# Second projection of a gated MLP on one NeuronCore: its seven block products in another order, signs moved into the operands, products of one quadrant added up in PSUM

## The chip, the cores and the metric

One core of a Trainium2 chip runs the whole kernel. The metric is device time in microseconds (us) of one execution. The engines are PE (TensorE: matrix products), DVE (VectorE), ACT (ScalarE), POOL (GpSimd) and SP (SyncE, which here only issues transfers). POOL also issues transfers that add to what is already at their destination. PEld is PE's loading of weights.

## The reference

One transformer layer over 1024 positions and 1024 channels: a norm, an input projection, a pooling mixer and chunked attention, an output projection; then the part that the change touches, and a gate at the end.

```
hn = rmsnorm(h, norm_ffn_g)
gt, val = split(hn @ w_up)                       # D_FF = 2816 each
gt = causal_dwconv(gt, conv_w, conv_b)           # width 3
h  = h + (gelu(gt) * val) @ w_down               # second projection: 2816 -> 1024
hn = rmsnorm(h, norm_ple_g)
h  = h + sigmoid(hn @ w_ple_gate + b_ple_gate) * (p @ w_ple)
out = rmsnorm(h, final_g)
```

## The kernel before, in words

Everything is held transposed: channels on the 128 partitions, positions along the row. H[d] is the residual of channel block d (0 to 7), 1024 positions in two halves HS[0], HS[1]. Each fp32 operand is split into two fp32r parts, hi (rounded, on ACT) and lo (the rest, on DVE), and each product is three matmuls: hi by hi, hi by lo, lo by hi (`mm3`, lines 128 to 130). The split is line 133 (ACT) and line 134 (DVE).

The up projection runs over 22 blocks of 128 of the 2816 channels. Block fi ends with `values_in` and a write of its 128 x 1024 result to the DRAM tensor GD[fi] (L869). Its last block uses the PSUM banks 0 to 3.

The second projection is a 2x2 block product done with seven products in place of eight (Strassen's way): the halves are those of the 22 blocks of the inner dimension, of the 1024 output channels, and of the 1024 positions. A product n is 11 steps (k = 0 to 10); step k multiplies a 128 x 512 weight form by a 128 x 512 form of the intermediate result, for four output blocks j of 128 channels: 4 x 3 = 12 matmuls of 512 columns, added up over k in four PSUM banks (`set_of[n]`). One product is 132 matmuls. The names:

- T(k), B12(k), B22(k): blocks of GD in SBUF (regions R0/R1, R2, R3). T is changed in place by sums on DVE as products go by.
- SW(k): sums of weight blocks in region R4. Its first block is a plain load; each further one is added by a transfer that POOL issues (`grown`, L892). Below, a1(k) is the accumulation that makes SW(k) for product 5, a2(k) the one that turns it into that of product 6, a3(k) that of product 3. Product 7 has weight sums of its own, in the raw buffers in F.
- `w_form` (four) and `g_form` (three): rings of split operands, so step i can be split once step i-4 (weights) or i-3 (the other side) is through PE.
- `raw_buf("w")` is a ring of six buffers for weight blocks, `raw_buf("g")` one of five for blocks of GD, "q" one of four for the gate's weights.

What sets the order: PE runs its instructions in program order. For DVE, ACT, POOL and SP a scheduler fixes the order when the program is built; each engine then runs its list strictly in order, and an instruction whose data is not there holds up all behind it. SP and POOL issue transfers in that order too. A transfer on SP's queue waits until the one eight places ahead has landed (its semaphore is one of eight in turn), so at most eight are under way.

`operands(n, k)` loads what step k of product n needs, six steps ahead (READY); `formed` splits it two steps ahead (FORMED); `behind` makes the sums that follow a split; `taken(n, j, ps)` adds the finished bank j to H. In the kernel before, the order of the products is 1, 2, 5, 6, 7, 4, 3, and the four `taken` of a product stand together right behind its last step:

```python
            if k == NK - 1:
                for j in range(4):
                    taken(n, j, PS[:, set_of[n][j]])
```

During the last products the weights of the gate are loaded and split (`gate_weights`), and the first half of the normalised residual (`weighted2`).

Of the kernel before, what the change touches and what calls it, by code (L numbers as in the profile page):

```python
# [83 lines left out]
def trunk(tc, xT, pT, vecs, w_qk0, w_in, w_v, bias, counts, pool_w, w_out, w_up, w_down,  # L84
# [4 lines left out]
    with tc.tile_pool(name="sb", bufs=1) as sb, \  # L89
# [795 lines left out]
        def gated(k, i, j):  # L885
            return GD[k + NK * (i - 1), :, (j - 1) * 512:j * 512]
# [20 lines left out]
        def U(j):  # L907
            return r(56 + 2 * j, 512)

        def operands(n, k):  # L910

            if n == 1:
                return load_to(raw_buf(), weight(k, 1, 1)), load_to(T(k), gated(k, 1, 1))
            if n == 2:
                load_to(B12(k), gated(k, 1, 2))
                return load_to(raw_buf(), weight(k, 1, 2)), load_to(raw_buf("g"), gated(k, 2, 1))
            if n == 5:
                load_to(B22(k), gated(k, 2, 2))
                grown(load_to(SW(k), weight(k, 2, 1)), k, 2, 2)
                return SW(k), T(k)  # L920
            if n == 6:
                return SW(k), T(k)
            if n == 7:
                t = grown(load_to(raw_buf(), weight(k, 2, 1)), k, 1, 1)
                b21[k] = load_to(raw_buf("g"), gated(k, 2, 1))
                return t, B12(k)
            if n == 4:
                return load_to(raw_buf(), weight(k, 2, 2)), T(k)
            return SW(k), load_to(raw_buf("g"), gated(k, 2, 2))

        def behind(n, k):

            tt = dve.tensor_tensor
            if n == 2:
                tt(T(k), T(k), B12(k), ALU.add)
            elif n == 5:
                tt(T(k), T(k), B22(k), ALU.subtract)
                grown(SW(k), k, 1, 1)
            elif n == 6:
                tt(B12(k), B12(k), B22(k), ALU.subtract)  # L940
                grown(SW(k), k, 1, 2)
            elif n == 7:
                tt(T(k), T(k), b21.pop(k), ALU.subtract)

        pinned, b21 = [False], {}
        sequence = [(n, k) for n in (1, 2, 5, 6, 7, 4, 3) for k in range(NK)]
        READY, FORMED = 6, 2
# [7 lines left out]
        def formed(upto):  # L955
            while made[1] < min(upto, len(sequence)):
                i = made[1]
                w_, g_ = got.pop(i)
                split(g_, *g_form[i % 3])
                split(w_, *w_form[i % 4])  # L960
                behind(*sequence[i])
                made[1] += 1
# [11 lines left out]
        rings["g"] = [r(b, 512) for b in range(118, 128, 2)]  # L974


        wg = []
# [14 lines left out]
        norm_b = Norm(HS[1], f(52.25, 512), [f(54.25, 512)], 4, 1)  # L992
# [10 lines left out]
        def taken(n, j, ps):  # L1003

            if n == 1:
                act.activation(U(j), ps, AF.Copy)
            elif n == 2:
                h_add(j, 0, ps)
                norm_a.add(j)
            elif n == 5:  # L1010
                h_add(4 + j, 1, ps)
                h_add(j, 1, ps, ALU.subtract)
            elif n == 6:
                dve.tensor_tensor(U(j), U(j), ps, ALU.subtract)
                h_add(j, 1, U(j), ALU.subtract)
            elif n == 7:
                dve.tensor_tensor(U(j), U(j), ps, ALU.add)
                h_add(4 + j, 0, U(j), ALU.subtract)
                h_add(4 + j, 1, U(j))
                norm_b.add(4 + j)  # L1020
            elif n == 4:
                h_add(4 + j, 0, ps, ALU.subtract)
                norm_a.add(4 + j)
            else:
                h_add(j, 1, ps)
                norm_b.add(j)

        set_of = {1: (0, 1, 2, 3), 2: (0, 1, 2, 3), 5: (4, 5, 6, 7), 6: (0, 1, 2, 3), 7: (4, 5, 6, 7),
                  4: (0, 1, 2, 3), 3: (7, 4, 5, 6)}

        def all_weights():
            for z in (2, 3):
                Rs[z] = region(z, F32R)
            wg.extend(r(32 + 8 * k, 2048) for k in range(KT))

        def first_half_forms():
            for z in (0, 1):
                Rs[z] = region(z, F32R)
            hp[0] = [(r(4 * k, 512), r(4 * k + 2, 512)) for k in range(KT)]

        extra = {(7, 10): all_weights, (4, 10): first_half_forms,
                 (3, 5): norm_a.sums, (3, 7): lambda: norm_a.rows(rst2[:, HS[0]])}
        for k, at in enumerate(((4, 1), (4, 3), (4, 5), (4, 7), (4, 9), (3, 1), (3, 3), (3, 4))):
            extra[at] = lambda k=k: gate_weights(k)

        for i, (n, k) in enumerate(sequence):
# [3 lines left out]
            for j in range(4):  # L1050
                js = slice(j * P, (j + 1) * P)
                mm3(PS[:, set_of[n][j]], whi[:, js], wlo[:, js], ghi, glo, k == 0 and n != 2, k == NK - 1, n == 2)
            if k == NK - 1:
                for j in range(4):
                    taken(n, j, PS[:, set_of[n][j]])
            if (n, k) in extra:
                extra[n, k]()
            if n == 3 and 1 <= k <= 8:
                weighted2(0, k - 1)
# [6 lines left out]
        Rs[4] = region(4, F32R)  # L1066
        pt = [(r(96 + 8 * k, 1024), r(100 + 8 * k, 1024)) for k in range(2)]
        wp = [(r(112 + 8 * k, 1024), r(116 + 8 * k, 1024)) for k in range(2)]
# [48 lines left out]
        for i in range(NG * KT):  # L1117
            g, d = i // KT, i % KT
            gate_mm(d, g, (7, 2, 3)[i % 3])
# [8 lines left out]
            for z in ((0, 1) if i == 1 else (i,)):  # L1128
                gz, dz = z // KT, z % KT
                ple_mm(dz, gz, ple_banks[z % 2])  # L1130
                gate_out(dz, gz, (7, 2, 3)[z % 3], ple_banks[z % 2], zt[z % 4])
# [63 lines left out]
```

## Time and profile before

| | |
|---|---|
| median of 3 runs | 1157.6 us (1156.49 to 1161.36) |
| the profiled execution | 1160.69 us, its span 1158.6 us |
| PE busy over the span | 1129.9 us (98%) |
| DVE, ACT, POOL busy | 902.0, 583.5, 250.5 us |
| clock of PE granted, mean | 0.993 |
| second projection, first to last matmul | 802.45 to 1031.8 us of the span |

The timeline lists instructions by their start; the bracket at a row's end gives the idle time ahead of it and what ended that. Rows that follow one another on DVE overlap a little: a row reads 0.69 us, while four in a row take 2.49. A row of several equal instructions carries their number (x2). The view by windows gives, for each stretch of time, its length and the busy time of each engine with the number of instructions.

### The profile page before, as it was taken

The page shows a single profiled execution, that of the slowest core. Times are in us where ns is not written, and L with a number is a line of the kernel's source. Part 1 is how long each engine was busy: PE and PEld are TensorE (multiplying, and loading weights), DVE is VectorE, ACT ScalarE, POOL GpSimd, SP SyncE. Part 2 cuts the span into 40 slices and gives each one's busy share as a digit, 9 for nine tenths or more (in the row PEclk, how much of TensorE's full clock was granted, in tenths as well). Part 3 has the DMA queues.
Part 4 walks back from the last instruction along what each step waited for, and adds up shares of the span by engine and source line. Part 5 has one row for each costly group of instructions (what it writes and reads, how often), then busy time and mean ns, then how long its engine had stood idle before and what let it go on. Part 6 is the DMA issues. An engine that isn't in the chain of part 4 may idle for free.

```text
span 1158.6 us, 15610 instructions
## 1 busy us (share of the span) xinstructions
PE 1129.9 (98%) x5697; PEld 956.1 (83%) x5697; DVE 902.0 (78%) x1408; ACT 583.5 (50%) x1023; POOL 250.5 (22%) x224
## 2 busy tenths in 40 slices
PE   8999999999999999999999999998999999999996
PEld 7988998888888778888888888887877777888996
DVE  7678878779557678999998999998669767984554
ACT  8568677764655444343434343444534435773332
POOL 0000000083012213343434343332023420000000
PEclk9999999999999999999999999999999999999998
DMA  7110102104510352212131312123999894610011
GB/s 262 37 49 30 49 12 67 39 28 157 171 28 10 69 145 77 103 62 102 64 103 64 105 64 101 64 101 109 322 295 255 149 223 127 209 47 1 26 66 56
DMA packets 58828, 117.22 MB, mean 101 GB/s; under 512 B 6656, under 2 KB 8960, under 8 KB 58752
## 3 DMA queue, kind: packets, MB, share of 16 engines
q1 hardware_dynamic: 50544, 101.48, 25.8%
q0 software_dynamic: 8064, 14.68, 7.6%
q8 instruction: 44, 0.72, 0.3%
q14 instruction: 32, 0.26, 0.1%
q10 hardware_dynamic: 144, 0.07, 0.0%
HBM read 100.48 MB, written 15.73 MB: 100 GB/s over the span
## 4 chain that ended last, share of the span: by engine, by line
PE 81%; issue 6%; DVE 4%; DMA 4%; ACT 2%; POOL 1%; SPq 0%; DVEq 0%; POOLq 0%; ACTq 0%
PE PS L129 24%; PE PS L128 24%; PE PS L130 24%; PE PS L366 2%; DMA R<-GD 2%; PE PS L384 1%; PE PS L383 1%; POOL R L892 1%; DMA R<-in_w_down 1%; DVE B L134 1%; DMA F<-in_w_up 1%; PE PS L341 1%; PE PS L340 1%; DVE F L1001 0%; DMA F<-in_w_qk 0%
## 5 line engine op out<-in xcount | busy, mean ns | idle before, releaser
L128 PE MATMUL PS<-R,R 128*128 128x512 f32 (+1 forms) x896 | 346.3, 386 | 3.1 <-ACT V L796 1.7
L130 PE MATMUL PS<-R,R 128*128 128x512 f32 (+1 forms) x896 | 343.2, 383 | 0.0
L129 PE MATMUL PS<-R,R 128*128 128x512 f32 x832 | 324.9, 390 | 0.3 <-DVE R L229 0.3
L134 DVE TENSOR_TENSOR R<-F,R 128x512 fp32r<-128x512 f32 (+1 forms) x214 | 190.6, 898 | 23.5 <-ACT R L133 22.9
L133 ACT ACTIVATE R<-F 128x512 fp32r<-128x512 f32 (+1 forms) x218 | 132.3, 621 | 140.9 <-PE PS L129 82.3
L128 PEld LDWEIGHTS PS<-R,R 128*128 128x128 f32 x896 | 168.6, 188 | 34.8 <-ACT V L796 2.1
L130 PEld LDWEIGHTS PS<-R,R 128*128 128x128 f32 x896 | 168.5, 188 | 33.5 <-DVE R L134 0.5
L710 POOL TENSOR_TENSOR F<-F 128x512 f32<-128x512 f32 x76 | 143.2, 1884 | 221.4 <-DVE R L134 142.4
L129 PEld LDWEIGHTS PS<-R,R 128*128 128x128 f32 x832 | 156.6, 188 | 31.1 <-DVE R L229 0.9
L129 PE MATMUL PS<-B 128*128 128x512 f32 x316 | 125.3, 396 | 8.8 <-DVE B L134 8.8
L128 PE MATMUL PS<-B 128*128 128x512 f32 x316 | 124.8, 395 | 3.1 <-DVE V L821 2.1
L130 PE MATMUL PS<-B 128*128 128x512 f32 x316 | 124.3, 393 | 0.0
L133 ACT ACTIVATE B<-R 128x512 fp32r<-128x512 f32 x110 | 65.1, 620 | 40.2 <-DMA R<-in_w_down 20.6
L134 DVE TENSOR_TENSOR B<-R,B 128x512 fp32r<-128x512 f32 x110 | 72.6, 687 | 14.4 <-ACT B L133 14.3
L129 PEld LDWEIGHTS PS<-B 128*128 128x128 f32 x316 | 60.1, 190 | 24.9 <-DVE B L134 12.5
L128 PEld LDWEIGHTS PS<-B 128*128 128x128 f32 x316 | 60.0, 190 | 16.9 <-DVE V L821 2.6
L129 PE MATMUL PS<-B,R 128*128 128x256 f32 x256 | 72.3, 282 | 0.0
L130 PEld LDWEIGHTS PS<-B 128*128 128x128 f32 x316 | 60.0, 190 | 12.5
L133 ACT ACTIVATE B<-F 128x512 fp32r<-128x512 f32 (+1 forms) x53 | 35.1, 663 | 67.6 <-PE PS L129 49.2
L352 ACT ACTIVATE F<-F,small 128x640 f32<-128x640 f32 (+2 forms) x64 | 44.4, 693 | 21.1 <-DVE small L350 12.8
L128 PE MATMUL PS<-B,R 128*128 128x256 f32 x192 | 54.6, 285 | 0.0
L130 PE MATMUL PS<-B,R 128*128 128x256 f32 x192 | 54.4, 283 | 0.0
(165 smaller groups left out, 1965.4 us busy)
## 6 DMA issues: line engine op xcount, KB each, us to landing
F<-in_w_up SPq DMA_DIRECT2D x91, 256.0 KB, 2.7
R<-GD SPq DMA_DIRECT2D x66, 256.0 KB, 5.3
GD<-F SPq DMA_DIRECT2D x22, 512.0 KB, 2.6
F<-in_w_down SPq DMA_DIRECT2D x44, 256.0 KB, 5.2
R<-in_w_down POOLq DMA_DIRECT2D x33, 256.0 KB, 6.7
F<-in_w_in SPq DMA_DIRECT2D x10, 512.0 KB, 3.8
F<-in_xT SPq DMA_DIRECT2D x16, 256.0 KB, 6.0
F<-in_w_out SPq DMA_DIRECT2D x16, 256.0 KB, 2.9
```

What stands on the lines that cost most here:

```text
L128: pe.matmul(ps, ahi, bhi, start=first, stop=False, skip_group_check=more)
L129: pe.matmul(ps, ahi, blo, start=False, stop=False, skip_group_check=more)
L130: pe.matmul(ps, alo, bhi, start=False, stop=last, skip_group_check=more)
L133: act.activation(hi, src, AF.Copy)
L134: dve.tensor_tensor(lo, src, rv(hi), ALU.subtract)
L340: pe.matmul(PS[:, 4 + z, 0:320], q, K2[:, ks], start=True, stop=False)
L341: pe.matmul(PS[:, 4 + z, 0:320], q, K1[:, ks], start=False, stop=True)
L352: act.activation(S[:, 0:n], S[:, 0:n], AF.Exp, bias=s_[:, 0:1], scale=-1.0, accum_out=s_[:, 1:2])
L366: pe.transpose(pst[:, j * P:(j + 1) * P], S[:, j * P:(j + 1) * P], ident)
L383: pe.matmul(O, V[:, k, h], pt[:, 0, idx], start=n_ == 0, stop=False)
L384: pe.matmul(O, V[:, k, h], pt[:, 1, idx], start=False, stop=n_ == len(ks) - 1)
L710: pool.tensor_tensor(rawu[to], rawu[a], rawu[b], op)
```

## The change: what it does

1. The order of the products is 1, 5, 6, 3, 7, 2, 4. The halves of the positions are swapped in what GD block is called 1 or 2, so the sums go to other quadrants of H.
2. Products 6, 7 and 4 go on adding in the banks 4 to 7 that product 1 began, product 3 in the banks 0 to 3 that product 5 began (`on_top`): their first matmul doesn't clear the bank. Where a quadrant needs a product with the other sign, the operand is split with a factor of -1 (`split_neg`, products 5 and 6).
3. Each finished bank is added to H once: 28 additions on DVE in place of 40, and no copy by ACT; the four of a product are written behind the steps 1, 3, 5 and 7 of the next one (`emptied`).
4. The blocks that product 3 and the sum behind product 2 need are not loaded a second time: 22 loads of 256 KB fewer. B12(k) is loaded in product 1: the first seven together, ahead of the weights of step 6.
5. Sums in place (`later_sums`) are made four steps after the split that they follow (LAG).
6. The gate's weights, the norm's forms and the last operands go to other regions; the gate's weights are loaded in products 7 and 2. Banks of the gate's products are named in another turn, and the norm's in other banks.

```diff
-            return GD[k + NK * (i - 1), :, (j - 1) * 512:j * 512]
+            return GD[k + NK * (i - 1), :, HS[2 - j]]
...
             if n == 1:
+                if pinned[0]:
+                    for z in range(0 if k == READY else k, k + 1):
+                        load_to(B12(z), gated(z, 1, 2))
                 return load_to(raw_buf(), weight(k, 1, 1)), load_to(T(k), gated(k, 1, 1))
-            if n == 2:
-                load_to(B12(k), gated(k, 1, 2))
-                return load_to(raw_buf(), weight(k, 1, 2)), load_to(raw_buf("g"), gated(k, 2, 1))
             if n == 5:
+                grown(load_to(SW(k), weight(k, 2, 1)), k, 2, 2)
                 load_to(B22(k), gated(k, 2, 2))
-                grown(load_to(SW(k), weight(k, 2, 1)), k, 2, 2)
                 return SW(k), T(k)
...
+            if n == 3:
+                return SW(k), B22(k)
...
+        def later_sums(n, k):
...
+        def split_neg(src, hi, lo):
+            act.activation(hi, src, AF.Copy, scale=-1.0)
+            dve.scalar_tensor_tensor(lo, src, -1.0, rv(hi), ALU.mult, ALU.subtract)
...
-        sequence = [(n, k) for n in (1, 2, 5, 6, 7, 4, 3) for k in range(NK)]
-        READY, FORMED = 6, 2
+        ORDER = (1, 5, 6, 3, 7, 2, 4)
+        sequence = [(n, k) for n in ORDER for k in range(NK)]
+        READY, FORMED, LAG = 6, 2, 4
...
+        set_of = {n: (4, 5, 6, 7) if n in (1, 6, 7, 4) else (0, 1, 2, 3) for n in ORDER}
+        on_top = (6, 7, 4, 3)
...
+            if k in (1, 3, 5, 7) and emptied:
+                emptied.pop(0)()
             if k == NK - 1:
                 for j in range(4):
-                    taken(n, j, PS[:, set_of[n][j]])
+                    emptied.append(lambda n=n, j=j: taken(n, j, PS[:, set_of[n][j]]))
```

What the change moves in the engines' lists is shown at three places.

SP's queue behind the write of the last block to GD (L869). F<-in_w_down is a weight block, R0 and R1 are T, R2 is B12. Before:

```order
L869 DMA GD_75<-F_70 128x1024
L880 DMA F_70<-in_w_down 128x512
L880 DMA R0_5998<-GD_75 128x512
L880 DMA F_70<-in_w_down 128x512
L880 DMA R0_5998<-GD_75 128x512
L880 DMA F_70<-in_w_down 128x512
L880 DMA R1_6067<-GD_75 128x512
```

and now:

```order
L869 DMA GD_75<-F_70 128x1024
L880 DMA R2_6068<-GD_75 128x512 x7
L880 DMA F_70<-in_w_down 128x512
L880 DMA R0_5998<-GD_75 128x512
L880 DMA R2_6068<-GD_75 128x512
L880 DMA F_70<-in_w_down 128x512
L880 DMA R0_5998<-GD_75 128x512
```

Seven loads of B12 stand ahead of the weight block and T of step 6, and one more in each step from there.

POOL's list of accumulations into SW. A row that waits for DVE is an a2: it needs the split of SW(k) for product 5 behind it; the others are a1. Before:

```order
L892 DMA R4_6070<-in_w_down 128x512 [waits DMAHW3_49]
L892 DMA R4_6070<-in_w_down 128x512 [waits DMAHW5_49,DMASW7_49]
L892 DMA R4_6070<-in_w_down 128x512 [waits DMAHW7_49]
L892 DMA R4_6070<-in_w_down 128x512 [waits DMAHW1_49,DMASW1_49]
L892 DMA R4_6070<-in_w_down 128x512 [waits DMASW4_49,DVE_49]
```

and now:

```order
L893 DMA R4_6070<-in_w_down 128x512 [waits DMAHW4_49]
L893 DMA R4_6070<-in_w_down 128x512 [waits DMASW7_49,DMASW4_49,DVE_49]
L893 DMA R4_6070<-in_w_down 128x512 [waits DMAHW6_49]
L893 DMA R4_6070<-in_w_down 128x512 [waits DMASW5_49,DMASW1_49,DVE_49]
L893 DMA R4_6070<-in_w_down 128x512 [waits DMAHW0_49]
```

The first row of both is a1(2). Before, a1(3), a1(4) and a1(5) follow, and a2(0) after them; now a2(0) stands ahead of a1(3), a2(1) ahead of a1(4), and so on: of the 18 rows up to a1(10) seven are an a2, and a1(10) is the 14th row behind a2(0).

DVE's list where one product ends and the next is under way: before, product 6 to 7. L134 is the lo part of a split; R2_6068 in L1014 and L1001 is the buffer U.

```order
L134 TENSOR_TENSOR B3_3430<-R2_6068,B3_3430 128x512
L1014 TENSOR_TENSOR R2_6068<-R2_6068,PS_74 128x512 x2
L1001 TENSOR_TENSOR F_70<-F_70,R2_6068 128x512 x2
L1014 TENSOR_TENSOR R2_6068<-R2_6068,PS_74 128x512 x2
L1001 TENSOR_TENSOR F_70<-F_70,R2_6068 128x512 x2
L134 TENSOR_TENSOR B3_3430<-R2_6068,B3_3430 128x512 x2
```

and now, product 3 to 7 (L1012 is the addition to H, R4_6908 the gate's weights, L610 the norm):

```order
L134 TENSOR_TENSOR B3_3430<-R2_6068,B3_3430 128x512
L1012 TENSOR_TENSOR F_70<-F_70,PS_74 128x512 x2
L134 TENSOR_TENSOR R4_6908<-V_3016,R4_6908 128x512
L134 TENSOR_TENSOR B3_3430<-R2_6068,B3_3430 128x512
L134 TENSOR_TENSOR B3_3430<-F_70,B3_3430 128x512
L134 TENSOR_TENSOR R4_6908<-F_70,R4_6908 128x512
L610 TENSOR_TENSOR F_70<-F_70 128x512
L1012 TENSOR_TENSOR F_70<-F_70,PS_74 128x512
```

Eight instructions that wait for the end of a product stood in one piece between two splits; now two stand there, and the others between later splits.

104 lines of the change are left out of this document (52 added, 52 removed).

## The prediction, as recorded ahead of the run

> **What bounds the kernel now.** I read the busy times first, then the second projection cut into its seven products (windows), then the timelines of PE, DVE, SP, ACT and POOL around the places where PE stood.
>
> ```profile
> span 1158.6 us, 15610 instructions
> PE 1129.9 (98%) x5697; PEld 956.1 (83%) x5697; DVE 902.0 (78%) x1408; ACT 583.5 (50%) x1023; POOL 250.5 (22%) x224
> ```
>
> PE is the bound, so a change pays by what PE waits. The windows are products 1, 2, 5, 6, 7, 4, 3 (columns: PE, PEld, DVE, ACT, POOL, clock, DMA share, GB/s):
>
> ```profile
> 802.44:836.12 33.68, 30.54 (x133) 24.62 (x132) 24.62 (x35) 15.95 (x26) 0.00 (x0) 1.00 0.71 246
> 836.12:866.04 29.92, 29.92 (x133) 24.78 (x132) 19.74 (x32) 13.19 (x24) 5.22 (x6) 1.00 0.95 294
> 866.04:900.10 34.06, 30.86 (x133) 24.48 (x132) 29.88 (x49) 14.57 (x27) 13.07 (x15) 1.00 1.05 249
> 900.10:931.12 31.02, 30.79 (x133) 24.56 (x132) 20.01 (x33) 12.69 (x23) 13.07 (x15) 1.00 0.89 155
> 931.12:966.26 35.14, 32.37 (x133) 25.72 (x132) 23.85 (x39) 12.70 (x23) 6.95 (x8) 0.95 0.84 208
> 966.26:1000.44 34.18, 31.54 (x133) 25.66 (x132) 31.64 (x52) 22.65 (x41) 0.00 (x0) 0.95 0.52 176
> 1000.44:1031.81 31.37, 31.37 (x146) 25.99 (x144) 26.81 (x45) 22.20 (x41) 2.02 (x1) 1.00 0.32 110
> ```
>
> Product 2 ran without a wait: 29.92 us, 2.72 a step, 0.227 a matmul. Seven of these are 209.4; the stage took 229.4. 1.45 of the rest are the norm's small matmuls (last window); 18.5 us are waits, all that can be had here. Their causes, from PE and DVE:
>
> ```profile
> 804.32 0.50 PE L128 MATMUL PS<-B 128*128 128x512 f32 x1 [1.01 <-DVE V L818]
> 808.11 0.50 PE L128 MATMUL PS<-B 128*128 128x512 f32 x1 [2.13 <-DVE V L821]
> 939.60 0.50 PE L129 MATMUL PS<-B 128*128 128x512 f32 x1 [2.39 <-DVE B L134]
> 974.73 0.79 PE L129 MATMUL PS<-B 128*128 128x512 f32 x1 [2.64 <-DVE B L134]
> ...
> 811.34 0.69 DVE L134 TENSOR_TENSOR B<-R,B 128x512 fp32r<-128x512 f32 x1
> 932.25 0.69 DVE L943 TENSOR_TENSOR R<-R,R 128x512 f32<-128x512 f32 x1 [4.62 <-DMA R<-GD]
> 966.59 2.49 DVE L1001 TENSOR_TENSOR F<-F,R 128x512 f32<-128x512 f32 x4
> 970.80 2.49 DVE L1001 TENSOR_TENSOR F<-F,R 128x512 f32<-128x512 f32 x4
> ```
>
> Product 1 waits for the up projection's banks (L818, L821). Product 7 waits for a split that stands behind a late GD block and eight evacuations, product 4 for one behind twelve.
>
> **What the change does, part by part.**
>
> *Evacuations.* 28 additions for 40, four ACT copies fewer: at 2.49/4 = 0.62 us this is 7.5 us of DVE, off the path but for the bursts. As the list shows, at most three stand together now (1.9 us), and a split has two steps (5.4 us) of lead. So the waits of products 7 (35.14 - 29.92 = 5.2) and 4 (4.3) should go, and the 1.1 of product 6, whose a2 stood behind accumulations for product 7 and now leave during product 5: -10.6. In their new places these products run at 29.92. What could be late next is DVE in product 2: 22 splits, 11 subtractions, 8 gate splits, 8 additions and norm sums are 49 x 0.62 = 30.4 us against 29.92; the lead takes up 0.5. At 0.69 each it would be 33.8 and +3.9: I take 0, and keep 3.9 as the end. Negated splits (another DVE operation), accumulating over two products (the same 924 matmuls), the smaller regions and the gate's turn of banks: 0, covered by 4 to 10 us of idle DVE a product; the 126.8 us behind the stage keep their instructions. The 22 loads saved cost PE nothing where they were, beyond the late GD block already counted.
>
> *Start of product 1.* It now uses the banks 4 to 7, so 33.68 - 29.92 = 3.8 us of waiting go. But DVE's list up to the split of T(3) is the same: it ends at 811.34 + 0.69 = 812.0, and step 3 would start at 802.45 + 3 x 2.72 = 810.6: +1.0 (0 to 1.4). Then step 6. SP's queue and ACT:
>
> ```profile
> 811.45 0.32 SPq L869 DMA_DIRECT2D GD<-F  x1
> 811.82 0.42 SPq L880 DMA_DIRECT2D F<-in_w_down  x1
> 816.81 0.43 SPq L880 DMA_DIRECT2D R<-GD  x1
> 817.50 0.33 SPq L880 DMA_DIRECT2D F<-in_w_down  x1
> 825.98 1.00 SPq L880 DMA_DIRECT2D R<-GD  x2
> ...
> 817.52 0.63 ACT L133 ACTIVATE B<-F 128x512 fp32r<-128x512 f32 x1 [2.32 <-DMA F<-in_w_down]
> 860.65 1.16 ACT L133 ACTIVATE B<-R 128x512 fp32r<-128x512 f32 x2 [4.36 <-DMA R<-in_w_down]
> ```
>
> The weights of step 6 were first behind the write (issued 811.82, there at 817.5: 5.7 us). Now they are eighth, T(6) ninth: the rows in those places were issued at 816.81 and 817.50. With 5.7 us T(6) lands at 823.2; two splits of 0.63 and 0.69 more, 824.5 at most, 823.6 if loads flow better; I take 824. Step 6 could have begun at 802.45 + 1.0 + 16.3 = 819.8: +4.2 of waiting, and a slow stretch behind it (below). Product 1 ends at 824 + 13.6 = 837.6 to 839.2, later than before (836.12). The 3.8 gained are given back.
>
> *Product 5, now second.* Its SW(0) is the 22nd row behind the write, the place of the row at 825.98; landing 5.3 later (the page's median), 831.3. Then POOL:
>
> ```profile
> 853.45 0.89 POOL L892 DMA_DIRECT2D R<-in_w_down  x1 [60.61 <-DMA R<-in_w_down]
> 855.81 0.86 POOL L892 DMA_DIRECT2D R<-in_w_down  x1 [0.23 <-issue]
> 860.87 0.87 POOL L892 DMA_DIRECT2D R<-in_w_down  x1 [4.20 <-issue]
> 867.85 0.89 POOL L892 DMA_DIRECT2D R<-in_w_down  x1 [2.11 <-DVE B L134]
> 879.40 0.88 POOL L892 DMA_DIRECT2D R<-in_w_down  x1 [1.15 <-DVE R L937]
> 887.25 0.88 POOL L892 DMA_DIRECT2D F<-in_w_down  x1 [1.20 <-issue]
> 904.92 0.87 POOL L892 DMA_DIRECT2D R<-in_w_down  x1 [3.30 <-DVE F L1001]
> 926.92 0.86 POOL L892 DMA_DIRECT2D R<-in_w_down  x1 [0.78 <-issue]
> ```
>
> Three accumulations go out (853.45 to 855.81); the fourth leaves at 860.87, just when the first has landed (ACT's wait ends at 860.65). So POOL keeps three under way, and its pace is a third of their latency: 7.2 us while plain loads run (2.4 apart; 867.85 to 887.25 are 8 gaps, 2.42), 1.69 apart without them (904.92 to 926.92, 13 gaps; 5.1 us). The row at 867.85 shows POOL standing for a split, as each a2 must.
>
> Now: a1(0) issued 831.3, landed 838.6, split by 839.9, a2(0) at 840.3. From there a1(10) is 14 rows on. How long do plain loads run beside it? 11 SW, 11 B22 and six blocks for product 7 are queued; 28 rows. SP's 22 rows from 811.45 to 825.98 were 0.66 apart; between 831.3 and 840.3, with three accumulations taking part of the engines, some eight land, so about 19 remain at 840. Their pace beside accumulations is
>
> ```profile
> 858.22 0.45 SPq L880 DMA_DIRECT2D R<-in_w_down  x1
> 881.64 0.33 SPq L880 DMA_DIRECT2D F<-in_w_down  x1
> ```
>
> 15 issues in 23.4 us, 1.56 each: 30 us, to about 868. So nearly all fourteen rows go at the slow pace: threes start at 840.3, 847.5, 854.8, 862, 869.2. a1(10), the third of the last, leaves at about 870.5 and lands in 5.5 at 876; 0.7 for its hi part, 2.72 for the step: product 5 ends at 879.4. Bounds: all gaps 1.69, 864.0 + 5.2 + 3.4 = 872.6; all 2.42, 874.2 + 7.2 + 3.4 = 884.8. Before, with a1(0) to a1(5) ahead of any a2 and thirteen us of lead, this product lost 4.1. Since it ends by the last accumulation, what PE lost in product 1 is swallowed.
>
> *Sum.* Second product over: 866.04 before, 879.4 now, +13.4. Then five products and the norm's matmuls: 5 x 29.92 + 1.45 = 151.05, against 1031.81 - 866.04 = 165.77 before, -14.7. Together -1.4 us; the stage ends at 1030.4. On the profiled execution's own 1160.7 that is 1159.3; the median of the three runs is 3.1 lower, so 1157.6 - 1.4 = 1156.2. With the ends above: -8.2 (1149.4) to +4.0 and 3.9 more in product 2 (1165.5).
>
> [...] The trace has accumulations at 5.1 and 7.2 us. [...]
>
> **Rivals.**
>
> A, accumulations keep the fast pace: the plain loads don't slow them. For it: 13 gaps of 1.69; fewer loads follow those of product 5 (six for product 7, where the last eleven of the fifteen above were for it). Against: the eight gaps of 2.42. It gives 872.6, -8.2: 1149.4. If accumulations are so short that they never hold PE, product 5 ends 29.92 behind its start at some 839.7, 869.6, and the sum is -11.2 (1146.4); of A's chance I give that 0.03, since no row is that short. [...]
>
> B, slower: at 879.40 to 887.25 three accumulations took 7.85 us. If that holds for all of product 5, a gap is 2.62: 840.3 + 36.6 + 7.9 + 3.4 = 888.2, +7.4: 1165.0. It is slower than noise from a pace of 2.5 us. Each wait over 2.3 us also costs a slow stretch: behind 2.39 us the matmuls come 0.43 apart, eight of them, +1.6:
>
> ```profile
> 940.29 0.63 PE L128 MATMUL PS<-B 128*128 128x512 f32 x1
> 940.72 0.63 PE L129 MATMUL PS<-B 128*128 128x512 f32 x1
> ```
>
> C, the waits of products 7 and 4 stay: the additions aren't spread in the list as the source has them (three together in front of products 6's, 3's and 4's third step), and one that waits for PE holds the splits. For it: L943 stood 4.62 us for a load. Against: 1.9 us in a lead of 5.4. It gives back 9.5: +8.1, 1165.7.
>
> **Numbers.** Forecast 0.61, A 0.21, B 0.11, C 0.07. Under 0.5% (5.8 us) is no change for a measurement of this kernel. The forecast's cases lie from -6 to +4; 0.03 of them count as faster and 0.02 as slower. Faster 0.21 + 0.03 = 0.24, slower 0.11 + 0.07 + 0.02 - 0.03 (a small B) = 0.17, the same 0.59. The range, 1149 to 1164, reaches to A and just short of B and C; about 0.2 lie outside.
>
> **What would show it.** Right: PE starts product 1 without a wait for banks and stands some 4 us at step 6; product 5 takes 38 to 42 us, waiting for splits of R4 behind accumulations some 2.4 us apart; products 6, 3, 7, 2, 4 take about 30 each, without a wait over 1 us. The steps fail singly if product 5 runs under 34 us (A), over 46 (B), or if a wait for L134 stands at the third step of a later product (C). The whole is wrong if POOL has more than three accumulations under way, or if product 1's loads land in another order than they are issued.

## The result, and the profile after

The changed kernel takes 1166.87 us (median of five, 1163.96 to 1167.99) where the kernel before takes 1156.74 us beside it: ratio 1.0075, 95% interval 1.005 to 1.0101. A second measurement gave 1.007 (1.0058 to 1.0082). By these ratios it is slower by 8 to 9 us, where a change of less than 5.8 us, to 1156.2 us, was forecast.

The page of the changed kernel, its first lines:

```profile
span 1162.2 us, 15566 instructions
...
PE 1133.5 (98%) x5697; PEld 957.3 (82%) x5697; DVE 896.2 (77%) x1396; ACT 581.6 (50%) x1019; POOL 249.7 (21%) x224
```

DVE has 5.8 us less to do and PE is busy 3.6 us longer with the same 5697 matmuls. The second projection, cut into its products 1, 5, 6, 3, 7, 2, 4 (windows of the changed kernel; columns as in the prediction):

```profile
800.90:837.50 36.60, 33.40 (x133) 26.40 (x132) 27.58 (x40) 13.10 (x21) 2.62 (x3) 0.91 0.78 265
837.50:880.79 43.29, 35.36 (x134) 25.96 (x132) 27.28 (x45) 13.75 (x25) 18.70 (x22) 0.92 1.01 225
880.79:911.00 30.21, 30.21 (x134) 24.71 (x132) 19.27 (x32) 12.70 (x23) 12.67 (x15) 1.00 0.87 140
911.00:940.92 29.92, 29.92 (x134) 24.79 (x132) 16.53 (x27) 12.66 (x22) 1.75 (x2) 1.00 0.11 33
940.92:972.52 31.60, 30.57 (x133) 24.64 (x132) 27.60 (x45) 21.11 (x38) 2.60 (x3) 1.00 0.70 203
972.52:1003.55 31.03, 30.26 (x134) 24.70 (x132) 28.63 (x47) 21.39 (x38) 0.00 (x0) 1.00 0.67 229
1003.55:1034.86 31.31, 31.31 (x145) 26.06 (x144) 23.10 (x39) 17.42 (x31) 1.43 (x1) 1.00 0.30 102
```

The stage takes 233.95 us against 229.4. Products 1 and 5 alone lose 36.6 + 43.3 - 2 x 29.92 = 20.1 us, more than all seven lost before (18.5), and only in them is the granted clock under 1.00 (0.91 and 0.92). The other five lose about 3 (154.1 us, of which 1.45 are the norm's matmuls, against 5 x 29.92).

Where PE stands, from its timeline:

```profile
820.94 0.79 PE L128 MATMUL PS<-B 128*128 128x512 f32 x1 [3.16 <-ACT B L133]
847.70 0.51 PE L128 MATMUL PS<-B 128*128 128x512 f32 x1 [1.80 <-ACT B L133]
854.79 0.80 PE L128 MATMUL PS<-B 128*128 128x512 f32 x1 [3.79 <-ACT B L950]
863.90 0.50 PE L128 MATMUL PS<-B 128*128 128x512 f32 x1 [0.39 <-ACT B L950]
865.22 0.50 PE L129 MATMUL PS<-B 128*128 128x512 f32 x1 [0.82 <-DVE B L951]
871.54 0.50 PE L128 MATMUL PS<-B 128*128 128x512 f32 x1 [0.81 <-ACT B L950]
872.35 0.50 PE L129 MATMUL PS<-B 128*128 128x512 f32 x1 [0.31 <-DVE B L951]
```

The first is step 6 of product 1. The others are the steps 3, 4, 6 and 8 of product 5. L950 and L951 are the negated split of T, not the split of the accumulated block SW (L133): the prediction had expected waits for SW alone. (On ACT T(4) stands right behind SW(4), a block of its own step, so the 3.79 us are still a wait for an accumulation; steps 6 and 8 are another matter, see the order on ACT.) Where the accumulations are, from POOL:

```profile
829.64 0.90 POOL L893 DMA_DIRECT2D R<-in_w_down  x1 [38.32 <-DMA R<-in_w_down]
838.23 1.76 POOL L893 DMA_DIRECT2D R<-in_w_down  x2 [5.30 <-DVE B L134]
845.26 0.89 POOL L893 DMA_DIRECT2D R<-in_w_down  x1 [3.75 <-DMA R<-in_w_down]
867.89 0.86 POOL L893 DMA_DIRECT2D R<-in_w_down  x1 [0.80 <-issue]
```

a1(0) leaves at 829.64, a2(0) at 838.23 behind a split, a1(10) at 867.89: from a2(0) on fourteen gaps of 2.12 us.

### The profile page after: what moved, and what is told of

Read it like the earlier page. It is cut to its first block, busy times and chain, and to the rows that moved or that the text cites. A ratio compares the mean times of both kernels' runs of the same rounds, so it can differ in the third digit from the quotient of the medians.

```text
span 1162.2 us, 15566 instructions
## 1 busy us (share of the span) xinstructions
PE 1133.5 (98%) x5697; PEld 957.3 (82%) x5697; DVE 896.2 (77%) x1396; ACT 581.6 (50%) x1019; POOL 249.7 (21%) x224
## 4 chain that ended last, share of the span: by engine, by line
PE 78%; DMA 7%; DVE 5%; issue 5%; ACT 2%; POOL 1%; SPq 0%; DVEq 0%; POOLq 0%; ACTq 0%
PE PS L129 23%; PE PS L128 23%; PE PS L130 23%; PE PS L366 2%; DVE R L134 2%; DMA R<-in_w_down 2%; PE PS L383 1%; PE PS L384 1%; DMA F<-in_w_up 1%; DMA R<-GD 1%; DMA F<-in_w_down 1%; DMA F<-in_w_gate 1%; POOL R L893 1%; DVE B L134 1%; PE PS L341 1%
## 5 line engine op out<-in xcount | busy, mean ns | idle before, releaser
L128 PE MATMUL PS<-R,R 128*128 128x512 f32 (+1 forms) x944 | 361.9, 383 | 1.6 <-ACT V L796 1.5
L130 PE MATMUL PS<-R,R 128*128 128x512 f32 (+1 forms) x944 | 358.0, 379 | 0.0
L129 PE MATMUL PS<-R,R 128*128 128x512 f32 (+1 forms) x880 | 340.1, 387 | 0.3 <-DVE R L229 0.3
L134 DVE TENSOR_TENSOR R<-F,R 128x512 fp32r<-128x512 f32 (+1 forms) x214 | 189.6, 893 | 26.6 <-ACT R L133 25.9
L130 PEld LDWEIGHTS PS<-R,R 128*128 128x128 f32 x944 | 177.6, 188 | 34.0 <-DVE R L134 0.4
L128 PEld LDWEIGHTS PS<-R,R 128*128 128x128 f32 x944 | 177.7, 188 | 33.8 <-ACT V L796 2.0
L133 ACT ACTIVATE R<-F 128x512 fp32r<-128x512 f32 (+1 forms) x218 | 132.3, 621 | 142.8 <-PE PS L129 81.5
L129 PEld LDWEIGHTS PS<-R,R 128*128 128x128 f32 x880 | 165.7, 188 | 32.2 <-DVE R L229 1.1
L134 DVE TENSOR_TENSOR B<-R,B 128x512 fp32r<-128x512 f32 x88 | 59.4, 686 | 36.5 <-ACT B L133 36.2
L133 ACT ACTIVATE B<-R 128x512 fp32r<-128x512 f32 x88 | 53.8, 623 | 61.0 <-PE PS L129 31.6
L352 ACT ACTIVATE F<-F,small 128x640 f32<-128x640 f32 (+2 forms) x64 | 44.4, 694 | 21.0 <-DVE small L350 12.8
L608 ACT ACTIVATE F<-F 128x512 f32<-128x512 f32 (+1 forms) x49 | 27.8, 568 | 47.8 <-DVE F L1112 24.3
```

Of the source, the lines that this page charges most:

```text
L128: pe.matmul(ps, ahi, bhi, start=first, stop=False, skip_group_check=more)
L129: pe.matmul(ps, ahi, blo, start=False, stop=False, skip_group_check=more)
L130: pe.matmul(ps, alo, bhi, start=False, stop=last, skip_group_check=more)
L133: act.activation(hi, src, AF.Copy)
L134: dve.tensor_tensor(lo, src, rv(hi), ALU.subtract)
L352: act.activation(S[:, 0:n], S[:, 0:n], AF.Exp, bias=s_[:, 0:1], scale=-1.0, accum_out=s_[:, 1:2])
```

## The experiments

Each run was timed against the kernel before. The table sums them up: time in us of product 1, of product 5, of the whole second projection (each product from PE's first matmul to that of the next one, so a wait ahead of a product's first matmul counts for the product before it), and the ratio to the kernel before with its 95% interval.

| kernel | product 1 | product 5 | stage | ratio |
|---|---|---|---|---|
| before (two traces) | 33.7, 34.2 | 34.1, 34.3 | 229.4, 229.6 | 1 |
| changed, first measurement | 36.6 | 43.3 | 234.0 | 1.0075 (1.005 to 1.0101) |
| e5_repeat: the same | 37.0 | 44.9 | 236.7 | 1.007 (1.0058 to 1.0082) |
| e4_no_first_sums | 36.8 | 29.9 | 222.1 | 0.9941 (0.9918 to 0.9964) |
| e1_b12_behind | 33.0 | 47.3 | 234.5 | 1.0068 (1.0046 to 1.009) |
| e2_a1_first | 37.5 | 36.2 | 228.0 | 0.9985 (0.9973 to 0.9997) |
| e10_forms_in_order | 36.9 | 32.5 | 223.6 | 0.9967 (0.9952 to 0.9981) |
| e3_scratch | 36.1 | 42.4 | 233.8 | 1.0042 (1.0027 to 1.0056) |
| e6_both_edits (e1 + e2) | 33.3 | 39.9 | 227.8 | 0.9996 (0.9982 to 1.0009) |
| e14_all_three (e1 + e2 + e10) | 34.0 | 36.6 | 226.2 | 0.9978 (0.996 to 0.9996) |
| e11_gate_splits_later | 37.2 | 44.4 | 234.4 | 1.0055 (1.0034 to 1.0077) |
| e8_spread_alone (on the kernel before) | 34.5 | 34.9 | 224.3 | 0.9966 (0.9949 to 0.9983) |
| e7_product2_second | 31.1 | 32.8 | 225.5 | 0.9975 (0.9962 to 0.9988) |
| e9_sums_in_order (e7 mended) | 30.9 | 31.8 | 216.7 | 0.9911 (0.9889 to 0.9932) |
| e12_combined | 30.5 | 31.7 | 214.5 | 0.990 (0.9879 to 0.9921) |

**Is it the accumulations of product 5?** One edit leaves them out:

```
-                grown(load_to(SW(k), weight(k, 2, 1)), k, 2, 2)
+                load_to(SW(k), weight(k, 2, 1))
```

> Edit: the changed kernel without the eleven first accumulations (W22 onto W21) of product 5; its left operand is then W21 alone, so that part of the weights' sum is left out of the computation; everything else stays. Theory (product 5's loss is these accumulations): product 5 runs at 30 to 31 us instead of 43.3, the stage ends 12 to 13 us earlier, the whole is 12 to 13 us faster than the changed kernel: 1154. Rival (the plain loads of SW and B22, late behind seven B12 blocks and the weights, hold product 5 as well): product 5 takes 34 us or more, with waits that end with loads on SP's queue, and the whole is 1158 or more.

Product 5 takes 29.93 us, as the first theory had it. Its window in this run:

```profile
838.28:868.21 29.93, 29.93 (x134) 24.79 (x133) 29.62 (x50) 12.76 (x23) 12.03 (x15) 1.00 1.04 239
```

The DMA engines are as busy as with them (share 1.04 against 1.01), and PE waits for no plain load. The 13.4 us that product 5 loses come with its first accumulations. The whole took 1153.6 us, as expected; the stage is 11.9 us shorter and not 13.4, since product 7 took 33.7 us in this trace. The window also shows DVE with 50 operations, 29.6 us, beside a product that doesn't wait: so many fit.

**Product 1.**

```
-                if pinned[0]:
-                    for z in range(0 if k == READY else k, k + 1):
-                        load_to(B12(z), gated(z, 1, 2))
-                return load_to(raw_buf(), weight(k, 1, 1)), load_to(T(k), gated(k, 1, 1))
+                w_t = load_to(raw_buf(), weight(k, 1, 1)), load_to(T(k), gated(k, 1, 1))
+                if k >= READY:
+                    load_to(B12(k - READY), gated(k - READY, 1, 2))
+                return w_t
             if n == 5:
+                if k < READY:
+                    load_to(B12(k + NK - READY), gated(k + NK - READY, 1, 2))
```

> Edit: the changed kernel with the seven loads of B12 no longer ahead of the weights of step 6; each B12 block is loaded behind the pair of a step, six steps later in the list. Theory (product 1's loss is the place of w6 and T(6) in SP's queue): T(6) is seven rows nearer to the write, 7 x 0.67 = 4.7 us earlier, so the wait of 3.3 us at step 6 and the slow stretch behind it (2.9 us) go: product 1 takes 30 to 31 us instead of 36.6. SW(0) leaves SP some 4 us earlier, so the accumulations start earlier by that, while PE reaches product 5 six us earlier: product 5 ends about 4 us earlier and takes 45 us instead of 43.3. Whole: 3 to 5 us faster than the changed kernel, about 1162. Rival (product 5's accumulations alone set the end, and their pace is held by the splits that the second accumulations wait for): product 1 shorter, product 5 longer by the same, the time stays at 1167. Second rival (B12 arrives late for the sums of T): a new wait in product 5, 1170 or more.

The wait at step 6 goes, as expected, and product 1 takes 3.6 us less. Its 33.0 us include 2.48 that PE now stands ahead of product 5's first step, for a1(0); product 5 itself takes 4.1 us more:

```profile
834.96 0.68 PE L128 MATMUL PS<-B 128*128 128x512 f32 x1 [2.48 <-ACT B L133]
```

The first rival was right: the time did not move (1.0068 against 1.007), since the end of product 5 hangs on its accumulations and not on its start. On top of the next edit (e2_a1_first) it gave nothing either:

> Edit: the two edits of e1_b12_behind and e2_a1_first together. Theory (with the first accumulations ahead of the second ones, the time saved in product 1 is no longer swallowed): product 1 31 to 33 us, product 5 36 to 38 us, the whole 3 to 5 us faster than e2_a1_first, ratio to the kernel before 0.995. Rival (product 5 is held by the start of the accumulations, which B12's loads only move): products 1 and 5 together stay at the 73.6 us of e2_a1_first, ratio 0.998.

Products 1 and 5 take 73.2 us together against 73.6 of e2_a1_first alone: the rival.

**The order on POOL.**

```
         def grown(dst, k, i, j):
-            pool.dma_start(dst, weight(k, i, j), accum_op=ALU.add)
+            ins = pool.dma_start(dst, weight(k, i, j), accum_op=ALU.add)
+            if pinned[0]:
+                tc.keep_in_program_order(ins)
...
         def behind(n, k):
-            if n == 5:
-                grown(SW(k), k, 1, 1)
...
         def later_sums(n, k):
                 tt(T(k), T(k), B22(k), ALU.subtract)
+                grown(SW(k), k, 1, 1)
```

> Edit: the changed kernel with POOL's accumulations kept in the order of the program, and the second accumulation into a block (W11 onto W21+W22) written four steps later, so that the first accumulations of steps 0 to 7 stand ahead of any second one, and product 7's stand behind all of product 6's. Theory (the 13.4 us that product 5 loses are first accumulations that queue behind second ones, each of which waits for a split that waits for PE): the first accumulations leave in threes 7.2 us apart from 829.6 on, the eleventh at about 855 and lands at 861; product 5 takes 31 to 34 us instead of 43.3, the whole is 9 to 12 us faster than the changed kernel, 1155 to 1158. Rival (the first accumulation starts too late in any order, and three under way are too slow for PE): a pace of 2.4 against 2.72 a step would not hold PE, but at 7.9 us of latency and loads beside it the fourth to sixth are still late: product 5 38 us or more, 1162 or more. Product 1 stays at 36 to 37 us by both.

Product 5 took 7.1 us less, and the whole is some 10 us faster than the changed kernel (0.9985 against 1.007). But it still took 36.2 us, more than expected: a1(8) to a1(10) still stood behind a2(0) to a2(2), and there is a second reason.

**The order on ACT.** The forms of the changed kernel stand on ACT in this order (from the order of its instructions; R0 is T, R4 is SW, a row with x2 is two blocks):

```
605 L133 ACTIVATE B3_3430<-R4_6070 128x512 x2     SW(3), SW(4)
606 L950 ACTIVATE B3_3430<-R0_5998 128x512        T(4)
607 L133 ACTIVATE B3_3430<-R4_6070 128x512        SW(5)
608 L950 ACTIVATE B3_3430<-R0_5998 128x512        T(5)
609 L133 ACTIVATE B3_3430<-R4_6070 128x512 x2     SW(6), SW(7)
610 L950 ACTIVATE B3_3430<-R0_5998 128x512        T(6)
```

T(6), long ready, stands behind SW(7), which waits for the accumulation of the step behind. The trace of the changed kernel shows SW(6), SW(7) and T(6) (the wait in front of the second is for a1(7)):

```profile
861.40 0.63 ACT L133 ACTIVATE B<-R 128x512 fp32r<-128x512 f32 x1 [3.14 <-DMA R<-in_w_down]
862.69 0.63 ACT L133 ACTIVATE B<-R 128x512 fp32r<-128x512 f32 x1 [0.66 <-DMA R<-in_w_down]
863.23 0.61 ACT L950 ACTIVATE B<-R 128x512 fp32r<-128x512 f32 x1
...
873.22 0.63 ACT L133 ACTIVATE B<-R 128x512 fp32r<-128x512 f32 x1 [1.73 <-DMA R<-in_w_down]
```

PE's waits at 863.90 and 865.22 end with the third row and its DVE half. In the same way T(8) stands behind SW(9), and PE's waits at 871.54 and 872.35 are for it. The four waits are 2.3 us. The last row is SW(10). The edit, on top of e2_a1_first, keeps the splits of product 5's left operands where the program has them:

```
+                if sequence[i][0] == 5:
+                    tc.keep_in_program_order(act.activation(w_form[i % 4][0], w_, AF.Copy))
+                    tc.keep_in_program_order(dve.tensor_tensor(w_form[i % 4][1], w_, rv(w_form[i % 4][0]), ALU.subtract))
```

> Edit: e2_a1_first with the splits of product 5's accumulated blocks kept in program order on ACT and DVE: the split of T(k) stands ahead of that of SW(k). In the changed kernel T(6) stands behind SW(7), and T(8) behind SW(9). Theory (a step of product 5 waits for the accumulation of the step behind it, because the split of its T stands behind that one's on ACT): the waits for L950 and L951 of the changed kernel go, product 5 takes 32 to 34 us instead of the 36.2 of e2_a1_first, ratio to the kernel before 0.996. Rival (the accumulations' own landing is what PE waits for, and the order on ACT only gives it another name): product 5 36 us, waits for L971 in place of L951, ratio 0.9985.

Product 5 took 32.5 us, 3.7 less; the ratio went from 0.9985 to 0.9967, with intervals that overlap. Its window:

```profile
839.29:871.81 32.52, 31.81 (x133) 24.34 (x133) 27.84 (x46) 13.88 (x25) 12.65 (x15) 1.00 1.06 250
```

**How many accumulations are under way.** Edit: dynamic_dma_scratch_size=1536 for 1024.

> Edit: the changed kernel with 1536 bytes instead of 1024 reserved for the descriptors of POOL's transfers; nothing else. Theory (POOL keeps three accumulations under way because its descriptors have no more room): four or five are under way, product 5's accumulations leave 1.5 to 1.8 us apart as far as no split holds them, product 5 takes 34 to 39 us instead of 43.3, whole 1158 to 1163. Rival (the three have another reason, or the splits hold POOL): POOL's list and product 5 stay as they are, 1167, and POOL's second accumulations are still at least 7 us behind the first of their block.

Three accumulations had gone by 831.67; then five left from 837.75 on, in 5 us, before POOL stood again (in the changed kernel three from 838.23 on, and the fourth at 845.26):

```profile
837.75 1.77 POOL L893 DMA_DIRECT2D R<-in_w_down  x2 [5.22 <-DVE B L134]
839.79 1.76 POOL L893 DMA_DIRECT2D R<-in_w_down  x2 [0.27 <-issue]
841.92 0.86 POOL L893 DMA_DIRECT2D R<-in_w_down  x1 [0.37 <-issue]
844.67 0.86 POOL L893 DMA_DIRECT2D R<-in_w_down  x1 [1.89 <-issue]
```

So the number under way went with this size: three at 1024, five at 1536. That its bytes are room for descriptors, and that these run out, is the theory's own reading; the trace shows only the number. But product 5 still took 42.4 us, above what the theory expected, and the whole gained only 3 us: the time to landing grew. POOL's transfers issued between 836 and 870 us (columns: count, size, median us from issue to landing), in the changed kernel:

```profile
R<-in_w_down POOLq DMA_DIRECT2D x15, 256.0 KB, 6.0
```

and with the larger room:

```profile
R<-in_w_down POOLq DMA_DIRECT2D x16, 256.0 KB, 9.5
```

With five under way in place of three each takes longer (9.5 us for 6.0); the pace up to a1(10) goes only from 2.12 to 1.86 us.

**The later products.**

> Edit: the changed kernel with the splits of the gate's weights two steps behind their loads, and kept there; loads where they were. In the changed kernel ACT stands 2.45 and 2.86 us in product 7 for these loads, with the splits of the next steps queued behind. Theory (this is what products 7 and 2 lose: 1.7 and 1.1 us): both take 29.9 to 30.2 us, the whole is 2 to 3 us faster than the changed kernel, ratio 1.004 to 1.005. Rival (the burst of gate splits, T sums and additions on DVE is the cause, and it only moves): one of the two stays above 31 us, ratio 1.007.

Edit: the gate's blocks are loaded where they were, and split two steps later. In the changed kernel ACT stands for them in product 7, with the forms of the next steps behind:

```profile
956.55 0.63 ACT L133 ACTIVATE R<-V 128x512 fp32r<-128x512 f32 x1 [2.45 <-DMA V<-in_w_gate]
961.75 0.63 ACT L133 ACTIVATE R<-F 128x512 fp32r<-128x512 f32 x1 [2.86 <-DMA F<-in_w_gate]
```

Product 7 went to 29.96 us, product 2 stayed at 31.37: theory for the one, rival for the other. Product 2's wait at step 4 (0.77 us in the changed kernel, for a split on DVE) is gone there, but six of its steps take 2.8 to 3.1 us; why is not settled. The ratio can't tell 1.0055 from 1.007.

**The spread additions alone**, in the kernel before:

> Edit: the kernel before, with its order, sums and loads, but the additions behind each product are spread over the second, fourth, sixth and eighth step of the next one, as the changed kernel has them (not behind products 1 and 3); U lies in another place. Theory (the waits of products 7 and 4, 5.2 and 4.3 us, came from the additions standing together in front of splits): both products take 30 to 31 us instead of 35.1 and 34.2, the whole is 7 to 10 us faster than the kernel before, ratio 0.991 to 0.994. Rival (the waits come from the late GD block and the accumulations, or the forty additions fill DVE wherever they stand): products 7 and 4 stay above 33 us each, ratio 0.997 or above.

```
+            if k in (1, 3, 5, 7) and emptied:
+                emptied.pop(0)()
```

The edit also puts the norm's sums in product 3 two to three steps later.

Products 4 and 6 ran at 29.92 us (before 34.2 and 31.0), but product 7 stayed at 33.84 of 35.1. So the additions were 5.6 us of the term in the products 7 and 4, not 9.5 (the stage is 5.1 us shorter). Product 6's 1.1 us can't be put down to the edit: in the second trace of the kernel before (e13_before_again) it ran at 29.92 without one. What is left in product 7 is an accumulated block of weights that comes late, as the rival said; ACT stands for it:

```profile
945.53 0.63 ACT L133 ACTIVATE B<-F 128x512 fp32r<-128x512 f32 x1 [7.45 <-DMA F<-in_w_down]
```

In the second trace of the kernel before product 7's longest wait (1.96 us, at step 6) is for a split behind a subtraction that stands for a late GD block, with no addition near it. The spreading pays on its own: 0.9966.

**Another order: product 2 second.** Product 2 needs no accumulated operand. The order 1, 2, 5, 6, 3, 7, 4 puts it ahead of product 5, so that product 5's sums can start earlier before they are needed.

> Edit: the changed kernel's sums in PSUM and spread additions kept, but the order is 1, 2, 5, 6, 3, 7, 4: product 2, whose operands need no sum, stands between 1 and 5. B12 is loaded with product 2, B22 behind the SW blocks, B21 a second time with product 7; POOL's accumulations keep the order of the program as in e2_a1_first. Theory (an accumulated operand that is needed 30 us after the first load costs nothing): product 1 30 to 31 us, product 2 30 to 31, product 5 30 to 32 without a wait for L133 over 1 us, the stage 214 to 219 us against 234, the whole 15 to 20 us faster than the changed kernel, ratio to the kernel before 0.987 to 0.992. Rival (three loads a step and the accumulations together are too much for the DMA engines): products 2 or 5 take 35 us or more, with waits that end with loads, ratio 0.995 or above. The additions of products 2 and 7 stand together again, in front of the next product: if that costs, waits for L134 show at the third step of 5 and 4, 2 to 5 us each.

Product 1 came as expected (31.1), but PE stood 5.8 us ahead of product 5:

```profile
871.00 0.77 PE L128 MATMUL PS<-B 128*128 128x512 f32 x1 [5.79 <-DVE F L1014]
```

On DVE, what stood ahead of the additions that PE waited for:

```profile
866.86 0.69 DVE L949 TENSOR_TENSOR R<-R,R 128x512 f32<-128x512 f32 x1 [2.08 <-DMA R<-GD]
870.17 2.48 DVE L1014 TENSOR_TENSOR F<-F,PS 128x512 f32<-128x512 f32 x4
```

The additions that empty product 2's banks (L1014) stood on DVE behind subtractions (L949) that waited for B22, which this version loads later. Neither theory had it. Kept where the program writes them (two subtractions in tc.keep_in_program_order):

> Edit: e7_product2_second with its subtractions of B22 (from T and from B12) kept where the program writes them on DVE; in e7 they stood ahead of product 2's additions to H and waited there for B22 loads until 868.4, and product 5's first matmul stood 5.8 us for those additions. Theory (that wait and the slow stretch behind it are all that e7 lost in products 2 and 5: 70.2 us against 59.8): products 2 and 5 take 60 to 62 us together, the stage ends 8 to 10 us earlier, ratio to the kernel before 0.988 to 0.990. Rival (the accumulations, which in e7 left between 850.5 and 876, hold product 5 as soon as PE is there earlier): product 5 takes 33 us or more with waits that end with loads of R4, ratio 0.993 or above.

Products 2 and 5 took 62.1 us together and the ratio is 0.9911, both just above what the theory expected. The first accumulations:

```profile
848.27 1.79 POOL L893 DMA_DIRECT2D R<-in_w_down  x2 [55.38 <-DMA R<-in_w_down]
```

That is 14.6 us ahead of product 5's first matmul (862.90); in the changed kernel it is 7.9 us (829.64, 837.50). So a lead of about half a product brought product 5 to 31.8 us; it didn't take the 30 us that the expectation of e7 speaks of. With the later gate splits too:

> Edit: e9_sums_in_order and the later gate splits of e11 together: the version that the runs so far point to. Theory: 2 to 3 us faster than e9_sums_in_order, every product at 30 to 31 us, the stage 212 to 215 us against the 229.4 of the kernel before, ratio 0.985 to 0.988. Rival (the additions of product 7 that stand together in front of product 4, and its eight gate pairs, fill DVE there): product 4 takes 34 us or more and the ratio stays that of e9.

```profile
801.78:832.31 30.53, 30.53 (x134) 24.62 (x132) 23.10 (x34) 13.64 (x23) 0.00 (x0) 1.00 0.72 255
832.31:863.07 30.76, 30.08 (x133) 24.62 (x132) 20.71 (x35) 12.77 (x23) 5.28 (x6) 1.00 0.98 307
863.07:894.79 31.72, 30.57 (x132) 24.77 (x133) 22.58 (x38) 14.66 (x27) 12.85 (x15) 1.00 1.06 251
894.79:924.72 29.93, 29.93 (x134) 24.78 (x133) 27.57 (x47) 12.70 (x23) 13.29 (x16) 1.00 0.93 160
924.72:954.63 29.91, 29.91 (x133) 24.77 (x132) 18.37 (x30) 12.81 (x23) 4.24 (x5) 1.00 0.42 87
954.63:984.55 29.92, 29.92 (x133) 24.66 (x132) 27.27 (x45) 21.38 (x39) 2.70 (x4) 1.00 0.83 237
984.55:1016.24 31.69, 31.69 (x145) 26.01 (x145) 28.78 (x48) 23.48 (x43) 1.42 (x1) 1.00 0.45 144
```

Products 1, 2, 5, 6, 3, 7, 4, all within 2 us of 29.92 (the last has the norm's matmuls). This version, 1147.5 us, beats both kernels: 0.990 (0.9879 to 0.9921). The stage, 214.5 us, is as expected, the ratio is not: 0.985 to 0.988 was. What the later splits add to e9 (0.6 us) is under what the runs can tell; the windows have it at 2.3 us.

**Does the changed kernel's order cost time by itself?** With all three edits on it, loads, accumulations and forms:

> Edit: the changed kernel, its order of products and all its sums, with the three edits of e1_b12_behind, e2_a1_first and e10_forms_in_order together. Theory (the loss lies in the order of product 2's place alone as far as the accumulations start too late for a product that comes second): product 1 31 to 33 us, product 5 34 to 36 us, both together 66 to 68 us where e10_forms_in_order has 69.4; ratio to the kernel before 0.994 to 0.996. Rival (late loads were the loss and nothing else): both together 61 to 63 us as in e9_sums_in_order, ratio 0.991.

Both theories missed: products 1 and 5 took 70.6 us together, where the two edits without B12's had 69.4 and e9 62.7. Product 5 in second place can't start before a1(0) has landed, however early PE gets there: here PE stands 2.32 us ahead of it.

**How far the traces carry.** A second trace of each kernel:

> The changed kernel once more, without an edit, beside the others of this job: its first five runs gave 1.0075 of the kernel before (1.005 to 1.0101), while its profiled execution lies only 3.3 us above that of the kernel before. Theory (some of the 8.7 us between the medians is the spread from run to run, and the traces show the true loss): ratio 1.003 to 1.006, product 1 about 36 us and product 5 about 43 us in a second trace too. Rival (the profiled execution was a lucky one): ratio 1.007 or more, and products 1 and 5 together 3 us or more longer than the 79.9 us of the first trace.

Products 1 and 5 were 2.0 us longer than in the first trace, between the two theories; the ratio, 1.007, is the rival's.

> The kernel before, without an edit, for a second trace. Theory (its first trace was of a slow execution, 1160.7 us where the median is 1156.7 to 1161, and the difference lies in the second projection's waits for loads and accumulations): products 1 and 5 are a few us shorter than 33.7 and 34.1 us, and the stage takes 225 to 228 us instead of 229.4. Rival (the difference lies outside the stage): the stage takes 229 us again, and the span differs ahead of it or behind it.

It was neither: the stage took 229.6 us and the span was 1159.1, nearly as in the first (229.4 and 1158.6). So the two kernels' traces differ by 3 to 7 us in span, their medians by 8 to 10. Over all versions the change of the whole (by the ratio, of 1158 us) lies 0 to 4 us above the change of the stage against 229.4 us, 1.5 in the mean. Part of what the traces don't show is due to which execution was traced: the first trace of the changed kernel is of the fastest of its five (1163.96 us), both traces of the kernel before are of longer ones (1160.7 and 1161.0 us, where its medians in these measurements are 1156.7 to 1161.1). Over 79 executions of the kernel before, timed beside the experiments, the length went with the granted clock: the six with a mean granted clock of 0.997 took 1154.6 to 1156.5 us, the thirteen with 0.991 took 1160.1 to 1164.1 us. What makes the clock of two executions of one kernel differ stays open.

## Why the prediction was wrong, step by step

The measured 1166.9 us lies 10.7 us above the forecast. The stage was forecast at 1030.4 - 802.45 = 228.0 us; the two traces have 234.0 and 236.7, 6.0 and 8.7 more; the rest is not located. Two steps of the prediction failed: that product 5 ends one step behind its last accumulation, and the size of the saving in the later products. In parts:

- *Start of product 1*: right in kind. No wait for banks, a wait of 3.16 us at step 6 (4.2 forecast), end at 837.5 (837.6 to 839.2 forecast). That the end agrees is in part luck: the product began 1.5 us earlier than before, and the slow stretch behind the wait took 2.9 us where 0 to 1.6 were allowed. Its 36.6 and 37.0 us are 0.6 and 1.0 above the forecast's 36.0, the middle of its range. That it is swallowed by product 5 was right too (e1_b12_behind).
- *Product 5, now second*: right in kind, too small: 41.0 forecast, 43.3 and 44.9 measured. The failed link is the last one, that the product ends by its last accumulation. Accumulations came at 2.12, not 2.42; a1(10) left at 867.9 (870.5 forecast), and ACT's wait for it ended at 873.2 (876). Then "0.7 for its hi part, 2.72 for the step" should have ended product 5 at 876.6. PE ended it at 880.8, because it was itself behind: PE's last waits are at 871.54 and 872.35, at step 8, and from there it still had three steps to do, without a wait for a1(10). It was behind for two reasons: T's forms stood behind SW's of later steps (2.3 us of waits in this trace, 3.7 us of product 5 by e10_forms_in_order on top of e2_a1_first), and the step that began at 854.79 took 5.67 us at half pace (last section). How much of the 4.2 us each made is not shown. In e10 the end comes 3.8 us behind the end of ACT's wait for a1(10), near the 3.4 of the sum. The order on ACT and DVE could have been read ahead of the result, as the order on POOL was.
- *Evacuations*: the mis-sized term. Products 6, 3, 7, 2, 4 and the norm were forecast at 151.05 us; they took 154.1 and 154.8. In the first trace product 7 gives 1.7 of it (gate loads on ACT, shown by e11_gate_splits_later), product 2 1.1 (not settled; it lies within the bound of 3.9 us for a full DVE), product 6 0.3. The term itself read product 7's old wait as one that goes with the additions; e8_spread_alone shortens the stage by only 5.1 us, since without that wait product 7 stands for a late block of weights. And the 1.1 us of product 6 were no lasting loss: the second trace of the kernel before doesn't have them.
- *Rivals.* B's price, 1165.0, is near the measured time, but B did not happen: its pace was 2.62, and the measured one, 2.12, is quicker than forecast. A's pace of 1.69 didn't come either, and C's place (L134 at the third step of a later product) shows no wait. Accumulations so short that they never hold PE, the case of 1146.4 us, are shown by no run: the median time to landing was 6.0 us in the changed kernel and 9.5 in e3_scratch (issues between 836 and 870 us).
- *Numbers*: the sum's own upper end, 1165.5 us, lay above the range given (to 1164). 0.59 for "the same" was too much, with two unknown queues (ACT's and DVE's) left out of the price of product 5, whose bounds (872.6 to 884.8) did hold the measured end.

## What to carry to other kernels

An operand that is summed by accumulating transfers wants a lead: put a product with plain operands in front of it before anything else is tuned. Here the lead went from 7.9 to 14.6 us; with product 5 second the best stage was 223.6 us (e10_forms_in_order), with product 2 in front of it 216.7 (e9_sums_in_order). When an operand comes late, read the order on every in-order engine for ready work that stands behind it: T's forms behind SW's, bank additions behind sums. A repair ahead of the wait that ends last moves nothing, as the loads of B12 showed (1.0068 without them in front, 1.007 with them).

## What was not expected of the hardware

PE's pace behind a wait. After the 3.16 us wait of product 1 twelve matmuls come at half pace or slower (the third, fourth and twelfth of them, and the first behind them); the granted clock over the product is 0.91, and 0.50 from 820.94 to 826.53:

```profile
822.26 0.63 PE L130 MATMUL PS<-B 128*128 128x512 f32 x1
822.69 0.63 PE L128 MATMUL PS<-B 128*128 128x512 f32 x1
...
826.10 0.63 PE L130 MATMUL PS<-B 128*128 128x512 f32 x1
826.53 0.44 PE L128 MATMUL PS<-B 128*128 128x512 f32 x1
```

0.43 us apart for 0.227, 5.6 us for a step of 2.72: this wait cost 3.2 us and then 2.9 more. It was the same behind the 3.79 us of product 5 (5.67 us a step, clock 0.50), and only some 0.4 us were lost behind the 1.80 at 847.70. The length of the wait doesn't decide it, and the prediction's 2.3 us is no bound: in product 7 of e8_spread_alone seven matmuls come at half pace behind a shorter wait,

```profile
946.73 0.51 PE L128 MATMUL PS<-B 128*128 128x512 f32 x1 [1.41 <-ACT B L133]
948.07 0.63 PE L130 MATMUL PS<-B 128*128 128x512 f32 x1
948.50 0.63 PE L128 MATMUL PS<-B 128*128 128x512 f32 x1
```

while in the kernel before none do behind the 2.13 us of product 1. What decides it is not shown.

With more accumulations under way (five for three, e3_scratch) their median time to landing rose from 6.0 to 9.5 us, and the time from one to the next fell only from 2.12 to 1.86 us.
